# FFN gate and up projections by Strassen's seven products

## Chip, core and metric

The kernel runs on one core of one Trainium2 chip. The time is that of the device for one execution, in microseconds; lower is better. Where a profile is shown, it is one execution recorded by the hardware profiler. TensorE is called PE, VectorE DVE, ScalarE ACT, GpSimd POOL, and the engine that issues most DMAs is SyncE, SP.

## What is computed

Two groups of 256 tokens with 1024 channels (512 tokens in all) pass through a trunk of two layers. Each layer is a half-step SwiGLU FFN, a token mixer, and a second half-step FFN. All data are float32. Per layer, cut to what matters here:

```
def swiglu(x, wg, wu, wd):
    return (jax.nn.silu(x @ wg) * (x @ wu)) @ wd          # wg, wu: 1024 x 2816; wd: 2816 x 1024

x = x + 0.5 * swiglu(rmsnorm(x, ffn1_norm[l]), ffn1_wg[l], ffn1_wu[l], ffn1_wd[l])
h = rmsnorm(x, mix_norm[l])
...                                                       # gated DeltaNet and differential attention on h @ w_in[l]
x = x + merged @ w_out[l]
x = x + 0.5 * swiglu(rmsnorm(x, ffn2_norm[l]), ffn2_wg[l], ffn2_wu[l], ffn2_wd[l])
```

So there are four FFNs, two in each layer.

## The kernel before

**Precision.** PE multiplies in the format fp32r, which keeps fewer bits than float32. Every operand is therefore split into a high part (rounded to fp32r) and a low part (what is left), and a product is the sum of three matmuls: high x high, high x low, low x high. `split` (L199 to L211) does this for weights: ACT casts the high part into a tile `wh` (L208), DVE subtracts it from the float32 weights into `wl` (L210). These tiles come from the pool `pw`, which has 4 buffers of each kind.

**Loads.** `wraw` (L190) issues one load of 1 MB from SP into a tile `raw`, of which there are 2 buffers; `wcols` loads 256 columns of a weight and splits them into two blocks of 128.

**A projection.** `proj` (L218 to L224) multiplies one block of 128 weight columns with the tokens: 8 blocks of 128 channels, three matmuls each, the weights standing in the array and up to 512 token columns moving through. The normalised tokens stand transposed in `xth` and `xtl`, [128, 8, 512], channels on the partitions. The result is one PSUM bank.

**The FFN.** `ffn` (L316) walks over the 22 blocks of 128 features in two chunks of 12 and 10, two blocks (a pair) at a time: gate and up weights of the pair are loaded and split, four projections follow, and `gate` (L317 to L323) makes silu(gate) x up and splits it into `hh` and `hl`. After each chunk `rowproj` (L270) multiplies with the chunk's rows of wd and adds into the token rows `x` (L281). The first pair of an FFN does its four projections for token group 0 first and then for group 1 (256 columns at a time), since group 1's normalised tokens are complete later. `norm_T` (L244) computes them: squares on ACT (L237), the scale on POOL (L229), transposes on PE (L260), high part on ACT (L263), low part on DVE (L264).

**What sets the order.** A scheduler lays the instructions of each engine out before the run, by readiness in its own model of time and by priority: program order, or ahead of it by an offset where the text says `high_priority` (AHEAD = 1500 for loads and splits). On the chip each engine then works its queue in that order and waits on semaphores; a tile's buffer is handed on when its last reader is done. So instructions of different projections can stand interleaved on PE.

**One accumulating DMA is there already**: L553, in the mixer, adds 512 KB from DRAM onto an SBUF tile, issued by POOL.

## Time and profile before

| | |
|---|---|
| median of 3 runs | 2378.45 us (2377.96 to 2379.27) |
| the profiled execution | 2379.84 us, span of its records 2378.1 us |
| PE busy | 2342.1 us, 98% of the span |
| DVE, ACT, POOL busy | 45%, 35%, 10% |
| moved by DMA | 242.36 MB, 102 GB/s on average |

How to read it: the span is cut by instruction records, engine by engine. "Busy" is the time in which an instruction of that engine was under way; matmuls are pipelined, so one begins before the last has ended, and the step from start to start tells their rate. PEld is the load of the standing operand, which runs beside the matmuls. An idle time is put down to what ended it (the releaser). A DMA's landing is the time from its issue to its completion. Names such as wh or raw are the program's tiles without their numbers, L208 a line of the kernel.

### The profile page before, as it was taken

To read this page: it belongs to the slowest core of one execution; us is meant where nothing else is said; L and a number is where in the kernel's file an instruction comes from. 1 tells how busy PE (TensorE), PEld (TensorE's weight loads), DVE (VectorE), ACT (ScalarE), POOL (GpSimd) and SP (SyncE) were. 2 spreads that over 40 slices of the span, in tenths; PEclk is the share of its full clock that TensorE was granted. 3 is DMA by queue.
4 is the path that set the end of the run, shared out by engine and by line. 5 is a ranking of instruction groups with operands and counts; after the bars stand their busy time and mean duration, and the time that the engine had idled before them with its cause. 6 is when DMAs were issued, how large, how long until landed. Compare 5 with 4: busy or idle time off the path is not lost.

```text
span 2378.1 us, 29279 instructions
## 1 busy us (share of the span) xinstructions
PE 2342.1 (98%) x12017; PEld 1992.6 (84%) x12017; DVE 1078.5 (45%) x1716; ACT 820.7 (35%) x1593; POOL 239.5 (10%) x235
## 2 busy tenths in 40 slices
PE   7999999999999999999999999999999999999998
PEld 7888888887899888888888888888878988888887
DVE  4333334677665433333343333356776554332333
ACT  4222234744433332222332222347344333322221
POOL 1000000124351000000000000001343400000000
PEclk9999999999999999999999999999999999999999
DMA  5323234732123223233323232356321242232322
GB/s 164 106 89 104 91 124 142 176 115 78 36 72 118 96 89 103 93 97 98 106 73 106 89 107 89 124 152 172 95 83 45 63 142 89 90 105 89 106 80 80
DMA packets 210390, 242.36 MB, mean 102 GB/s; under 512 B 15565, under 2 KB 175585, under 8 KB 210256
## 3 DMA queue, kind: packets, MB, share of 16 engines
q1 hardware_dynamic: 204800, 221.96, 29.4%
q0 software_dynamic: 5280, 18.33, 3.1%
q8 instruction: 94, 1.54, 0.3%
q14 instruction: 40, 0.33, 0.0%
q10 hardware_dynamic: 176, 0.20, 0.0%
HBM read 229.17 MB, written 11.30 MB: 101 GB/s over the span
## 4 chain that ended last, share of the span: by engine, by line
PE 91%; DVE 4%; DMA 2%; ACT 2%; issue 1%; SPq 0%; POOL 0%; DVEq 0%; POOLq 0%; ACTq 0%
PE ps L222 18%; PE ps L223 18%; PE ps L224 18%; PE ps L275 8%; PE ps L277 8%; PE ps L276 8%; PE ps L730 1%; PE ps L827 1%; PE ps L935 1%; PE ps L936 1%; PE ps L937 1%; PE ps L638 1%; DMA v<-gcd 1%; PE ps L860 1%; PE ps L397 1%
## 5 line engine op out<-in xcount | busy, mean ns | idle before, releaser
L222 PE MATMUL ps<-xth,wh 128*128 128x512 f32 (+1 forms) x2208 | 827.7, 378 | 5.1 <-ACT xth L263 2.7
L223 PE MATMUL ps<-xtl,wh 128*128 128x512 f32 (+1 forms) x2208 | 829.7, 377 | 1.8 <-DVE xtl L264 1.8
L224 PE MATMUL ps<-xth,wl 128*128 128x512 f32 (+1 forms) x2208 | 827.2, 377 | 0.0
L208 ACT CAST wh<-raw 128x1024 fp32r<-128x1024 f32 x366 | 384.6, 1051 | 1065.2 <-PE ps L223 744.3
L210 DVE TENSOR_TENSOR wl<-raw,wh 128x1024 fp32r<-128x1024 f32 x354 | 440.1, 1244 | 674.3 <-ACT wh L208 659.9
L222 PEld LDWEIGHTS ps<-xth,wh 128*128 128x128 f32 x2208 | 416.9, 189 | 80.8 <-ACT xth L263 4.4
L223 PEld LDWEIGHTS ps<-xtl,wh 128*128 128x128 f32 x2208 | 418.1, 189 | 73.9 <-DVE xtl L264 2.4
L224 PEld LDWEIGHTS ps<-xth,wl 128*128 128x128 f32 x2208 | 418.0, 189 | 73.0
L276 PE MATMUL ps<-wl,u 128*128 128x512 f32 x576 | 224.4, 389 | 0.0
L275 PE MATMUL ps<-wh,u 128*128 128x512 f32 x576 | 224.3, 390 | 0.0
L277 PE MATMUL ps<-wh,u 128*128 128x512 f32 x576 | 223.2, 390 | 0.0
L320 DVE TENSOR_TENSOR t<-t,ps 128x512 f32<-128x512 f32 x88 | 60.5, 688 | 267.7 <-PE ps L224 264.3
L277 PEld LDWEIGHTS ps<-wh,u 128*128 128x128 f32 x576 | 108.2, 188 | 22.5
L275 PEld LDWEIGHTS ps<-wh,u 128*128 128x128 f32 x576 | 108.2, 188 | 22.3
L276 PEld LDWEIGHTS ps<-wl,u 128*128 128x128 f32 x576 | 108.2, 188 | 22.3
L229 POOL TENSOR_TENSOR nr<-nst,mhalf 128x1 f32<-128x1 f32 x28 | 15.5, 555 | 940.9 <-DVE nst L241 940.9
L281 DVE SCALAR_TENSOR_TENSOR u<-ps,u 128x512 f32<-128x512 f32 x80 | 53.7, 688 | 78.0 <-PE ps L277 78.0
L237 ACT ACTIVATE P<-u 128x512 f32<-128x512 f32 x56 | 35.3, 631 | 117.8 <-DVE u L281 113.3
L361 POOL DMA_DIRECT2D xs<-u x8 | 4.6, 574 | 705.9 <-DVE u L281 705.9
L935 PE MATMUL ps<-u,wh 128*128 128x256 f32 x256 | 70.4, 285 | 1.9 <-DVE u L955 1.9
L936 PE MATMUL ps<-u,wh 128*128 128x256 f32 x256 | 71.3, 287 | 0.0
L937 PE MATMUL ps<-u,wl 128*128 128x256 f32 x256 | 70.3, 285 | 0.0
(292 smaller groups left out, 2558.0 us busy)
## 6 DMA issues: line engine op xcount, KB each, us to landing
raw<-in_ffn_wg_dram SPq DMA_DIRECT2D x44, 1024.0 KB, 5.3
raw<-in_ffn_wu_dram SPq DMA_DIRECT2D x44, 1024.0 KB, 5.3
raw<-in_w_in_dram SPq DMA_DIRECT2D x44, 1024.0 KB, 5.4
raw<-in_ffn_wd_dram SPq DMA_DIRECT2D x40, 1024.0 KB, 5.0
v<-in_masks_dram SPq DMA_DIRECT2D x16, 512.0 KB, 7.1
v<-gcd POOLq DMA_DIRECT2D x16, 512.0 KB, 9.9
raw<-in_w_out_dram SPq DMA_DIRECT2D x8, 1024.0 KB, 4.9
raw<-in_ffn_wd_dram SPq DMA_DIRECT2D x8, 512.0 KB, 3.7
```

Source lines behind the costliest of these rows:

```text
L208: A.copy(hi, rv)
L210: (G_ if share and turn[0] % 2 else V).tensor_tensor(lo, rv, hi.bitcast(F32), op=ALU.subtract)
L222: T.matmul(o, wh[:, k, m], xh[:, k, c0:c1], start=k == 0, stop=False)
L223: T.matmul(o, wh[:, k, m], xl[:, k, c0:c1], start=False, stop=False)
L224: T.matmul(o, wl[:, k, m], xh[:, k, c0:c1], start=False, stop=k == n - 1)
L275: T.matmul(ps, sh[:, a], wh, start=k == 0, stop=False)
L276: T.matmul(ps, sh[:, a], wl, start=False, stop=False)
L277: T.matmul(ps, sl[:, a], wh, start=False, stop=k == nk - 1)
L320: V.tensor_tensor(s, s, pu_, op=ALU.mult)
L935: T.matmul(ps[:, c], wh[:, k, m], h_, start=k == 0, stop=False)
L936: T.matmul(ps[:, c], wh[:, k, m], l_, start=False, stop=False)
L937: T.matmul(ps[:, c], wl[:, k, m], h_, start=False, stop=k == H - 1)
```

## The change

**The products.** Except for the first pair of each FFN, a pair's gate and up projections become one 2 x 2 block product by Strassen's scheme (in the form with shared sums). The weights' quarters are wg and wu (256 columns of each) by upper and lower half of the channels; the tokens' quarters are the two halves of the channels by the two token groups. Seven products of a [512 x 256] weight combination with a [512 x 256] token combination replace eight. Each product is 2 feature blocks x 4 channel blocks x 3 split terms of matmuls with 256 moving columns. The products are summed in three PSUM tiles X, E and Z, some with further terms added on PE (`start=False`) after DVE has read what stood there.

**Weight sums.** Two of them are made by DMAs of POOL that add onto an SBUF tile: wu's upper rows onto wu's lower rows (`t3`, two tiles), and wu's upper rows onto wg's upper rows in the loaded tile `w11`, after product 1's parts have been taken from it. DVE makes `t2` from `w11` and `w22`, and later adds `w21` to it.

**Token sums.** `combos`, once per FFN after the first pair's projections: copies of the four quarters by SP, the low parts added by accumulating DMAs of POOL, four subtractions on DVE, splits on ACT and DVE. Two of the combinations overwrite token group 1's quarters in `xth` and `xtl`.

**Chunks** of the features are now 8, 8 and 6 blocks, so `rowproj` runs three times per FFN.

**The start.** The first pair's weights are loaded in quarters (`raw0`) ahead of the second token group; 22 matmuls of zeros (`spin`) run before the tokens are there and 2 more in `norm_T`; group 1's squares are put behind the casts of the first weights.

The diff, cut to its core:

```diff
...
-        with tc.high_priority(offset=AHEAD // 2):
+            raw0 = []
+            for j in range(2):
+                for n in ("ffn1_wg", "ffn1_wu"):
+                    raw0.append(uv((P, 8, P)))
+                    nc.sync.dma_start(raw0[-1], I[n][0][:, j * P:(j + 1) * P].rearrange("(k p) n -> p k n", p=P))
             load_x(2)
             load_x(3)
         g1col = p1.tile([P, 16], F32, name="g1col")
...
+        idle = p1.tile([P, P], BF16, name="idle")
+        V.memset(idle, 0.0)
+        def spin(n, lhs=None, rhs=None):
+            lhs = idle if lhs is None else lhs
+            rhs = idle.rearrange("p (a b) -> p a b", a=1).broadcast_to([P, 4, P]) if rhs is None else rhs
+            ps = bank("a", tuple(rhs.shape))
+            for _ in range(n):
+                T.matmul(ps, lhs, rhs, start=True, stop=True)
+        with tc.high_priority(offset=3 * AHEAD):
+            spin(22)
...
-        def split(rv, dst=None, share=False):
+        def split(rv, dst=None, share=False, off=AHEAD):
...
-            with tc.high_priority(offset=AHEAD):
+            with tc.high_priority(offset=off):
                 A.copy(hi, rv)
...
-        def sq_half(t, d):
+        def sq_half(t, d, behind=None):
             if d == 0:
                 sq[t] = small(f"nss{t}", (2,))
+                if behind is not None:
+                    A.copy(sq[t][:, :1], behind)
             A.activation(dtmp("P", (P, TOK)), x[t][:, d * TOK:(d + 1) * TOK], AF.Square, accum_out=sq[t][:, d:d + 1])
...
-        def norm_T(g, gain, xT):
+        def norm_T(g, gain, xT, fill=None):
...
+                if fill is not None and j == 0:
+                    with tc.high_priority(offset=-40):
+                        spin(fill, a[0][:, :P], a[1])
...
-        def ffn(wg, wu, wd, xT, after, extra=None):
+        def ffn(wg, wu, wd, xT, after, extra=None, norm=None):
...
-            for f0, f1 in ((0, 12), (12, 22)):
+            xh, xl = xT
+            low, high, g0, g1 = slice(0, 4), slice(4, 8), slice(0, 256), slice(256, 512)
+            X11, X12 = [[t[:, k, g0] for t in xT] for k in (low, high)]
+            C = {}
+            def combos():
+                q = {}
+                for g, c in enumerate((g0, g1)):
+                    for k, r in enumerate((low, high)):
+                        q[g, k] = u((P, 4, 256))
+                        with tc.high_priority(offset=100):
+                            nc.sync.dma_start(q[g, k], xh[:, r, c].bitcast(F32))
+                            G_.dma_start(q[g, k], xl[:, r, c].bitcast(F32), accum_op=ALU.add)
+                sub = lambda o, i, j: V.tensor_tensor(o, i, j, op=ALU.subtract)
+                sub(q[1, 1], q[1, 0], q[1, 1])
+                sub(q[1, 0], q[1, 0], q[0, 0])
+                sub(q[0, 0], q[0, 0], q[1, 1])
+                sub(q[0, 1], q[0, 1], q[0, 0])
+                for n, f, dst in ((5, q[1, 1], [t[:, low, g1] for t in xT]), (6, q[0, 0], None), (7, q[1, 0], None), (3, q[0, 1], None)):
+                    hi, lo = C[n] = dst or [uv((P, 4, 256), F32R) for _ in range(2)]
+                    A.copy(hi, f)
+                    V.tensor_tensor(lo, f, hi.bitcast(F32), op=ALU.subtract)
+                C[4] = [t[:, high, g1] for t in xT]
+                for t in C[4]:
+                    A.activation(t, t.bitcast(F32), AF.Copy, scale=-1.0)
+            def parts_of(pieces):
+                hi = pw.tile([P, 4, 256], F32R, tag="whi", name=nm("wh"))
+                lo = pw.tile([P, 4, 256], F32R, tag="wlo", name=nm("wl"))
+                n = 4 // len(pieces)
+                for i, r in enumerate(pieces):
+                    split(r, (hi[:, n * i:n * i + n, :], lo[:, n * i:n * i + n, :]))
+                return hi, lo
+            def product(ps, w, act, start=True):
+                (wh, wl), (ch, cl) = w, act
+                for j in range(2):
+                    m, o = slice(j * P, (j + 1) * P), ps[:, j, :]
+                    for k in range(4):
+                        T.matmul(o, wh[:, k, m], ch[:, k, :], start=start and j + k == 0, stop=False, skip_group_check=True)
+                        T.matmul(o, wh[:, k, m], cl[:, k, :], start=False, stop=False, skip_group_check=True)
+                        T.matmul(o, wl[:, k, m], ch[:, k, :], start=False, stop=k == 3, skip_group_check=True)
+            def seven(f, hh, hl):
+                c = slice(f * P, f * P + 256)
+                rows = lambda w, k0, n: w[k0 * P:(k0 + n) * P, c].rearrange("(k p) n -> p k n", p=P)
+                with tc.high_priority(offset=AHEAD):
+                    r = pr.tile([P, 2048], F32, tag="raw", name=nm("raw")).rearrange("p (q k n) -> p q k n", q=2, k=4)
+                    w11, w22 = r[:, 0], r[:, 1]
+                    nc.sync.dma_start(w11, rows(wg, 0, 4))
+                    nc.sync.dma_start(w22, rows(wu, 4, 4))
+                    t3 = [dtmp(n, (P, 2, 256)) for n in "PM"]
+                    for i, t in enumerate(t3):
+                        nc.sync.dma_start(t, rows(wu, 4 + 2 * i, 2))
+                        G_.dma_start(t, rows(wu, 2 * i, 2), accum_op=ALU.add)
+                    w21 = [dtmp(n, (P, 2, 256)) for n in "RS"]
+                    for i, t in enumerate(w21):
+                        nc.sync.dma_start(t, rows(wg, 4 + 2 * i, 2))
+                sq_ = (P, 2, 256)
+                X, E, Z = bank("f", sq_), bank("d", sq_), bank("a", sq_)
+                product(X, parts_of([w11]), X11)
+                with tc.high_priority(offset=AHEAD):
+                    G_.dma_start(w11, rows(wu, 0, 4), accum_op=ALU.add)
+                    t2 = u((P, 4, 256))
+                    V.tensor_tensor(t2, w11, w22, op=ALU.add)
+                p1s, G = dtmp("C", sq_), dtmp("E", sq_)
+                A.copy(p1s, X)
+                product(E, parts_of([t2]), C[6])
+                V.tensor_tensor(G, E, p1s, op=ALU.subtract)
+                product(Z, parts_of([w11]), C[5])
+                product(E, parts_of(t3), C[7], False)
+                H, y22 = dtmp("B", sq_), tmp(sq_)
+                V.tensor_tensor(H, E, p1s, op=ALU.subtract)
+                V.tensor_tensor(y22, Z, H, op=ALU.add)
+                product(X, parts_of(w21), X12, False)
+                s0 = tmp(sq_)
+                A.activation(s0, X, AF.Silu)
+                with tc.high_priority(offset=AHEAD):
+                    for i, t in enumerate(w21):
+                        V.tensor_tensor(t2[:, 2 * i:2 * i + 2, :], t2[:, 2 * i:2 * i + 2, :], t, op=ALU.add)
+                product(Z, parts_of([w22]), C[3], False)
+                V.tensor_tensor(G, Z, G, op=ALU.add)
+                V.tensor_tensor(s0, s0, G, op=ALU.mult)
+                product(E, parts_of([t2]), C[4], False)
+                y21 = dtmp("B", sq_)
+                V.tensor_tensor(y21, p1s, E, op=ALU.subtract)
+                A.activation(y21, y21, AF.Silu)
+                V.tensor_tensor(y22, y21, y22, op=ALU.mult)
+                for v, g in ((s0, g0), (y22, g1)):
+                    hi, lo = hh[-1][:, :, g], hl[-1][:, :, g]
+                    A.copy(hi, v)
+                    V.tensor_tensor(lo, v, hi.bitcast(F32), op=ALU.subtract)
+            for f0, f1 in ((0, 8), (8, 16), (16, 22)):
                 hh, hl = [], []
                 for f in range(0, f1 - f0, 2):
-                    mem = u if f < 10 else uv
-                    hh.append(mem(dt=F32R))
-                    hl.append(mem(dt=F32R))
-                    gs = wcols(wg, (f0 + f) * P)
-                    us = wcols(wu, (f0 + f) * P)
-                    if f0 + f == 0:
-                        bs = [bank_alt() for _ in range(4)]
+                    hh.append(u(dt=F32R))
+                    hl.append(u(dt=F32R))
+                    if f0 + f:
+                        seven(f0 + f, hh, hl)
+                        continue
+                    bs = [bank_alt() for _ in range(4)]
+                    if norm is not None:
+                        ws = []
+                        norm(0)
+                        for i, (b, rv) in enumerate(zip(bs, raw0)):
+                            hi = pw.tile([P, 8, P], F32R, tag="whi", name=nm("wh"))
+                            lo = pw.tile([P, 8, P], F32R, tag="wlo", name=nm("wl"))
+                            if i:
+                                k = (3, 7, 7)[i - 1]
+                                A.copy(hi[:, 0, :1], xT[0][:, k, :1])
+                                V.tensor_copy(lo[:, 0, :1], xT[1][:, k, :1])
+                            ws.append(split(rv, (hi, lo), off=0 if i else AHEAD))
+                            proj(b, ws[-1], xT, 0, 256)
+                        norm(1, [w[0][:, 0, :1].bitcast(F32) for w in ws])
+                        for b, w in zip(bs, ws):
+                            proj(b, w, xT, 256, 512)
+                    else:
+                        gs, us = wcols(wg, 0), wcols(wu, 0)
                         for g in range(2):
                             for b, w in zip(bs, (gs[0], us[0], gs[1], us[1])):
                                 proj(b, w, xT, g * 256, g * 256 + 256)
-                        for j in range(2):
-                            gate(bs[2 * j], bs[2 * j + 1], f + j, hh, hl)
-                    else:
-                        for j in range(2):
-                            pg, pu_ = bank_alt(), bank_alt()
-                            proj(pg, gs[j], xT)
-                            proj(pu_, us[j], xT)
-                            gate(pg, pu_, f + j, hh, hl)
+                    combos()
+                    for j in range(2):
+                        gate(bs[2 * j], bs[2 * j + 1], f + j, hh, hl)
...
-        for g in range(2):
+        def first_norm(g, behind=()):
             for t in (2 * g, 2 * g + 1):
-                sq_half(t, 0)
+                sq_half(t, 0, behind[t] if behind else None)
                 sq_half(t, 1)
-            norm_T(g, gaincol(0, 0), xT)
+            norm_T(g, gaincol(0, 0), xT, 2 if g == 0 else None)
...
-            ffn(I["ffn1_wg"][l], I["ffn1_wu"][l], I["ffn1_wd"][l], xT, to_norm(1, l), load_params if l == 0 else None)
+            ffn(I["ffn1_wg"][l], I["ffn1_wu"][l], I["ffn1_wd"][l], xT, to_norm(1, l), load_params if l == 0 else None,
+                first_norm if l == 0 else None)
...
```

## Rows read from the trace of the kernel before

**Rows 1.** Page, part 1: busy time (share) and instructions of each engine.

```profile
PE 2342.1 (98%) x12017; PEld 1992.6 (84%) x12017; DVE 1078.5 (45%) x1716; ACT 820.7 (35%) x1593; POOL 239.5 (10%) x235
```

**Rows 2.** Page, part 4: engines on the chain that ended last.

```profile
PE 91%; DVE 4%; DMA 2%; ACT 2%; issue 1%; SPq 0%; POOL 0%; DVEq 0%; POOLq 0%; ACTq 0%
```

**Rows 3.** Windows, FFN stretch: length, busy time per engine (instructions), clock, DMA share, GB/s.

```profile
60.00:280.00 220.00, 220.00 (x972) 182.29 (x971) 72.41 (x77) 56.51 (x68) 0.00 (x0) 1.00 0.31 98
```

**Rows 4.** Timeline of PE (start, duration): first and last of 28 matmuls, 512 columns.

```profile
1239.72 0.39 PE L224 MATMUL ps<-xth,wl 128*128 128x512 f32 x1
...
1245.84 0.39 PE L224 MATMUL ps<-xth,wl 128*128 128x512 f32 x1
```

**Rows 5.** Same view, 256 columns: three of L222 together; first and last of 129.

```profile
29.75 0.52 PE L222 MATMUL ps<-xth,wh 128*128 128x256 f32 x3
...
30.71 0.28 PE L222 MATMUL ps<-xth,wh 128*128 128x256 f32 x1
...
46.07 0.28 PE L223 MATMUL ps<-xtl,wh 128*128 128x256 f32 x1
```

**Rows 6.** Lines by form: shapes, count | busy us, mean ns | idle before, releaser.

```profile
L210 DVE TENSOR_TENSOR wl<-raw,wh 128x1024 fp32r<-128x1024 f32 x354 | 440.1, 1244 | 674.3 <-ACT wh L208 659.9 <-PE ps L386 9.6 <-PE ps L224 3.9
...
L320 DVE TENSOR_TENSOR t<-t,ps 128x512 f32<-128x512 f32 x88 | 60.5, 688 | 267.7 <-PE ps L224 264.3 <-PE ps L165 3.4
...
L567 DVE TENSOR_TENSOR v<-v,ua 128x1024 f32<-128x1024 f32 x8 | 9.6, 1220 | 8.2 <-ACT v L559 8.2
...
L208 ACT CAST wh<-raw 128x1024 fp32r<-128x1024 f32 x366 | 384.6, 1051 | 1065.2 <-PE ps L223 744.3 <-PE ps L277 247.9 <-PE ps L936 39.7
...
L322 ACT CAST u<-t 128x512 fp32r<-128x512 f32 x80 | 49.7, 622 | 0.9 <-DVE t L320 0.9
```

**Rows 7.** DMA issues, us to landing: L553 alone (5.2 twice), all sixteen; a plain load.

```profile
v<-gcd POOLq DMA_DIRECT2D x1, 512.0 KB, 5.2
...
v<-gcd POOLq DMA_DIRECT2D x1, 512.0 KB, 5.0
...
v<-gcd POOLq DMA_DIRECT2D x1, 512.0 KB, 6.3
...
v<-gcd POOLq DMA_DIRECT2D x16, 512.0 KB, 9.9
...
raw<-in_ffn_wd_dram SPq DMA_DIRECT2D x8, 512.0 KB, 3.7
```

**Rows 8.** Windows while one accumulate runs alone; last columns: clock, DMA share, GB/s.

```profile
476.00:477.00 1.00, 1.00 (x6) 0.84 (x5) 1.00 (x2) 0.00 (x0) 0.00 (x0) 1.00 1.05 209
```

**Rows 9.** Waits: who waited for whom, us in total, times, longest.

```profile
ACT wh L208 <- PE ps L223: 744.3, 206, 8.0
```

**Rows 10.** Timeline of DVE at the third FFN: tokens complete; first pair ends.

```profile
1204.34 3.22 DVE L264 SCALAR_TENSOR_TENSOR xtl<-ps,g1col,xth 128x256 fp32r<-128x256 f32 x8 [3.03 <-ACT xth L263]
...
1223.19 0.69 DVE L320 TENSOR_TENSOR t<-t,ps 128x512 f32<-128x512 f32 x1 [0.76 <-PE ps L224]
```

**Rows 11.** Timeline of PE at the start: dense from here; first 512-column matmul.

```profile
19.74 0.58 PE L223 MATMUL ps<-xtl,wh 128*128 128x256 f32 x1 [1.17 <-DVE xtl L264]
...
46.31 0.40 PE L222 MATMUL ps<-xth,wh 128*128 128x512 f32 x1
```

**Rows 12.** Same stretch: slow steps, their end, six transposes; granted clock (windows).

```profile
20.34 0.42 PE L222 MATMUL ps<-xth,wh 128*128 128x256 f32 x1
...
24.18 0.42 PE L222 MATMUL ps<-xth,wh 128*128 128x256 f32 x1
...
25.85 0.37 PE L223 MATMUL ps<-xtl,wh 128*128 128x256 f32 x1
...
26.41 0.82 PE L260 MATMUL ps<-cst,R 128*128 128x128 f32 x6
...
20.00:25.00 5.00, 5.00 (x24) 5.00 (x25) 2.71 (x9) 1.26 (x5) 1.69 (x3) 1.00 0.80 269
```

**Rows 13.** Timeline of ACT at the start: first square of token group 1.

```profile
17.96 0.66 ACT L237 ACTIVATE P<-u 128x512 f32<-128x512 f32 x1
```

## Prediction

> **What bounds the kernel now.** Read the busy table first: TensorE 98% against 45% on VectorE (DVE) and 35% on ScalarE (ACT) [rows 1]. The chain that ended last runs 91% over PE [rows 2]. But "busy" is no proof of a full array, so read a stage next: in the feed-forward stretch from 60 to 280 us PE never pauses, DVE is busy 72.4 of 220 us, ACT 56.5, POOL nothing, the DMA engines 0.31 [rows 3]. Here only less PE time can help. The price of a matmul is not its 390 ns duration but the step from start to start: 28 matmuls of 512 columns, 6.12 us from first to last, 0.2267 us each [rows 4]; 129 of 256 columns, 15.36 us, 0.1200 us each [rows 5]. The difference, 0.1067 us, is 256 columns at 2.4 GHz; 0.0133 us per matmul is fixed and is paid however narrow it is.
>
> **1. The products.** A pair of feature blocks (256 columns of gate and of up) takes today 2 projections x 2 blocks x 8 row blocks x 3 split terms = 96 matmuls of 512 columns: 96 x 0.2267 = 21.8 us. Strassen takes 7 products x 2 x 4 x 3 = 168 of 256 columns: 168 x 0.1200 = 20.2 us. So 1/8 fewer columns give back only 1.6 us (7%), since the fixed part is paid 168 times. The first pair of each of the 4 FFNs stays as it is, so 10 pairs x 4 = 40 change: **-64 us** at most, if PE never waits. It waits for nothing today because DVE and ACT have twice the time they need; that cover is what the change spends.
>
> The Trainium skill says, in "TensorE: Matmul & The Clock Gate", section "Back-to-back issue gap", that in streams of weight load and matmul the step is about 131 ns at 512 columns and 81 ns at 128. In proportion between these, an estimate from that page, 256 columns would step at about 98 ns, and a pair would go from 12.6 to 16.4 us: the change would cost 155 us. The rows above do not agree with either figure, and they decide; what is true in it is that narrow matmuls pay their fixed part more often.
>
> **2. The other engines in a pair** [rows 6]. DVE today: 4 low parts x 1.244 + 4 x 0.69 = 7.7 us of 21.8. DVE after: 5 low parts of 1024 elements x 1.244, 4 of 512 x 0.69, the sum t2 1.22, its second sum 2 x 0.69, seven combinations x 0.69, two low parts of the result x 0.69 (512-element rows stand for all of these): 6.2 + 2.8 + 1.2 + 1.4 + 4.8 + 1.4 = 17.8 us of 20.2, 88%. ACT: 5 x 1.05 + 9 of 512 elements x 0.62 = 10.8 us, 54%. Loads: 2 MB plain and 1 MB accumulating in place of 2 MB. The stretch moved 98 GB/s at a share of 0.31 [rows 3], so 316 GB/s at full use: 6.6 us for 2 MB. No engine is over the PE's 20.2 us, but DVE is near it.
>
> **3. The wait that the change adds.** Product 1 needs w11; then POOL's DMA adds wu's upper rows onto the same buffer; then DVE makes t2 of it, t2 is split, and product 2 needs that. An accumulating DMA is in the trace already: L553 adds 512 KB onto a tile. Alone it lands 5.0 to 6.3 us after its issue, four such cases; the median of all sixteen, most of them queued behind each other, is 9.9 [rows 7]. While one ran alone the engines were full at 209 GB/s [rows 8], two thirds of the 316 above, so 1 MB takes them 5.0 us and a pair 11.6 of 20.2 us.
>
> How early may this begin? The split tiles have 4 buffers, and ACT's casts wait today mostly for PE to give one back [rows 9]; so product 1's split comes when the product four places before it is done, and product 2 starts 4 x 24 x 0.120 = 11.5 us later. In series, with the durations of [rows 6]: cast 1.05, low part 1.24, accumulate 5.1, sum 1.22, cast 1.05, low part 1.24 less the 0.24 that the first two matmuls cover: 10.7 us. It fits by 0.8 us if no step queues. Three of them queue on a DVE that is 88% busy with operations of 0.7 to 1.2 us, and the issue on POOL queues behind the two accumulates of t3; some 0.45 us a step, 1.4 us in all, so I take **0.6 us of PE wait**. The first changed pair after a down projection is spared (its splits each feed 24 matmuls x 0.2267 = 5.4 us, so four give 21.8 us of lead): 8 of 10 pairs wait, 32 in all: **+19 us**. Bounds: 0, since the order on PE is not the program's (the matmul of L223 runs ahead of L222 in places, three of one line in a row [rows 5], and other products can fill the gap), and 173 us, where it lands as late as that median: 9.9 - 5.1 on top of 0.6, 5.4 us a pair, x 32. I stay by the lone row since POOL issues only three of these per 20 us.
>
> The Trainium skill, "DMA: Bandwidth & Descriptors", section "Anatomy of one DMA — SWDGE (gpsimd) path", fits 2.0 us plus the bytes over 436 GB/s to such a DMA. For 512 KB that is 3.2 us, an estimate from the page; the lone accumulates take 5.0 and more, so trace and page differ. By the page this wait would vanish, and the sum would be 2317.
>
> **4. The combinations of the tokens** (once per FFN): 4 plain copies and 4 accumulates of 512 KB, 4 subtractions and 4 splits on DVE (4 x 1.22 + 4 x 1.24 = 9.8 us), 6 operations on ACT. At the start of the third FFN the second token group is complete at 1207.6, and the first pair ends just before its last gating, at 1223.2 [rows 10]. From 1207.6: copies 3.7 (as a plain 512 KB load [rows 7]), two accumulates about 7.6 (5.1 and 2.5 behind it), three subtractions 3.7: 1222.6. The parts for product 5 overwrite tokens that the first pair reads, so ACT casts from 1223.2 on, product 6's operand second: ready about 1226.5 where product 1 ends at 1226.1. With the first pair's gating queued on DVE too I take 2 us per FFN, **+8 us** (bounds 0 and 24: 6 us each if all of the DVE work were exposed). The down projection in 3 chunks instead of 2 adds 8 evacuations of 0.688 us on DVE per FFN and no matmul; DVE has two thirds of that stage free: 0.
>
> **5. The start.** Dense matmuls begin at 19.7 us and the first pair ends at 46.3 [rows 11]; 19 of them from 20.34 step at 0.2133 us, the pace of 256 columns at 1.2 GHz, up to 25.8 us; the granted clock reads 1.00 there, so the step tells it, not that column [rows 12]. ACT puts group 1's squares (17.96) between the parts of group 0 [rows 13]. The zero products run while PE has nothing else, the quarters of weights come early, and the squares move behind the casts. Six us at half pace cost 3; some 2 us of order come on top: **-5 us** (bounds 0 and -8: 192 x 0.120 plus 32 transposes x 0.11 [rows 12] after a start at 12 would end at 38.6). Moved on SP: two x loads fall behind four weight loads; they are needed only for group 1.
>
> **Sum.** The profiled run took 2379.84 us (span 2378.1): -64 + 19 + 8 - 5 = -42, 2337.8; the median of the runs lies 1.4 lower: **2336 us**.
>
> **Rivals.**
> - *All hidden* (2311 us, 0.25): the order on PE fills every gap; terms 3 and 4 fall to 0 and 2. For it: the rows out of order [rows 5]. Against: under 1 us of slack.
> - *The accumulate decides, slower* (2413 us, 0.17): shared with 2 MB of plain loads per pair it lands after 7.5 us, a wait of 3.0 us x 32 = 96 in place of 19. The point: the gain is spent when the wait reaches 61 / 32 = 1.9 us, which is a landing at 6.4 us. One lone case took 6.3.
> - *DVE's queue* (2381 us, 0.10): DVE works in order; if the sum t2 stands at its head for 4.0 of the 5.1 us that the DMA is under way, waiting and 17.8 us of work make 21.8 us, and a pair lasts what it lasted.
> - *Narrow matmuls don't keep their step* (2397 us, 0.03): 21.8 / 168 = 0.1295 us is the point; at 0.132 a pair costs 0.4 us more than today, x 40 = +16 in place of -64 and +19. Against: 129 rows at 0.1200.
>
> **How the numbers follow.** Forecast 0.45. Range: 2304 (all hidden, the start at -8, term 4 at 0, 2 us for the spread of runs) to 2395, a landing near 6.9 us, which leaves out most of the slower rival. A measurement can tell some 0.2%, 5 us, from no change. Faster: 0.45 + 0.25 + part of DVE's queue = 0.76; same 0.07; slower 0.17.
>
> **What would show it.** 168 matmuls per pair at 0.120 us; product 1 to product 1 in 20.2 us if hidden, 20.8 as forecast, 21.8 without gain. PE's idle time inside a chunk put down to t2's split (DVE or its cast), and behind it to the accumulate; landing near 5 us; DVE at some 85% in the pairs; PE idle under 10 us at each FFN's second pair; the first pair ending near 41 us. I am wrong if landing exceeds 6.4 us, if DVE waits at the head of its queue for a DMA, or if steps exceed 0.1295.

## The result and the profile after

The changed kernel takes 2536.11 us (median of 4 runs, 2534.26 to 2539.42) against 2378.68 us for the kernel before: a ratio of 1.0664 [1.0651, 1.0677], 157 us slower. The forecast was 2336 us and faster. Line numbers from here on are those of the changed kernel, unless a line is said to be of an experiment.

The page of the changed kernel, busy time, granted clock in 40 slices, and the engines on the chain that ended last:

```profile
PE 2357.6 (93%) x14923; PEld 2133.0 (84%) x14923; DVE 1498.2 (59%) x2304; ACT 1000.4 (40%) x1864; POOL 415.7 (16%) x371
...
PEclk8899999999999989999989989999999999899999
...
PE 75%; DVE 11%; DMA 6%; ACT 4%; issue 3%; POOL 1%; SPq 1%; POOLq 0%; DVEq 0%; ACTq 0%
```

Against [rows 1, 2], PE fell from 98% to 93% busy and from 91% to 75% of the chain, and the clock has slices at 8. So PE waits, and at times runs at its lower level. A busy sum can't part the two, so PE's time is counted from start to start of its matmuls. Columns at 2.4 GHz plus the 0.0133 us of [rows 4, 5] count as work. What a step takes beyond that counts as slow steps, or as standstill where it is more than 0.35 us. In us, for the four FFNs together (the whole PE stream for the mixers):

| kernel | time | work | slow steps | standstill |
|---|---|---|---|---|
| before | 2378.7 | 1449 | 12 | 11 |
| changed | 2536.1 | 1391 | 66 | 163 |

Work fell by 58, slow steps grew by 54, standstill by 152; the two mixers grew by 11 (their stages, 446.5 and 445.6 to 454.0 and 449.4) and the first matmul starts 4.5 us earlier: +154 us, and the spans of the two profiles differ by 154.0 (2532.1 against 2378.1). So slow steps and standstill are more than the whole loss. Of the slow steps, 7 of the 12 us before and 51 of the 66 after are steps at just the pace of 1.2 GHz; the other 15 of the 66 are smaller delays, 9 of them in the four steps behind a stop.

**Where PE stands.** The waits of the changed kernel (engine and tile, who was waited for: us in all, times, longest):

```profile
DVE E L431 <- PE ps L391: 148.4, 40, 5.5
...
PE ps L389 <- ACT wh L226: 129.0, 55, 17.0
...
ACT wh L226 <- DVE u L414: 91.0, 29, 9.5
...
DVE u L414 <- DMA raw<-in_ffn_wu_dram: 62.8, 9, 11.6
```

Read from the second line down: PE waits for a cast, the cast (29 times) for the sum t2 on DVE (L414), but t2 waits for the accumulating transfer only 9 times in 40 pairs. By landing times it had landed ahead of t2 in 29 of the others: by 0.2 to 5.5 us, in half of them by no more than 1.1, 47 us in all. So it was the queue that held t2 there, though in half of these pairs the transfer would have let it start only some 1 us earlier. The first line tells what DVE did meanwhile: 40 times it stood at L431, which needs product 6. One pair shows it, one of the worse (3.3 of these us); DVE from the timeline (start, duration, then line, operation, and in brackets the idle time before it):

```profile
220.07 0.69 DVE L423 TENSOR_TENSOR t<-ps,B 128x512 f32<-128x512 f32 x1
226.30 0.69 DVE L431 TENSOR_TENSOR E<-ps,E 128x512 f32<-128x512 f32 x1 [5.54 <-PE ps L391]
227.10 0.69 DVE L432 TENSOR_TENSOR t<-t,E 128x512 f32<-128x512 f32 x1
227.98 0.69 DVE L435 TENSOR_TENSOR B<-C,ps 128x512 f32<-128x512 f32 x1 [0.19 <-PE ps L391]
228.58 0.68 DVE L441 TENSOR_TENSOR u<-t,u 128x512 fp32r<-128x512 f32 x1
229.18 1.22 DVE L414 TENSOR_TENSOR u<-raw 128x1024 f32<-128x1024 f32 x1
```

The same pair on ACT, POOL (the issue of the accumulate) and PE:

```profile
216.34 1.05 ACT L226 CAST wh<-raw 128x1024 fp32r<-128x1024 f32 x1 [1.79 <-PE ps L390]
...
230.44 1.04 ACT L226 CAST wh<-u 128x1024 fp32r<-128x1024 f32 x1 [1.11 <-DVE u L414]
...
218.95 1.30 POOL L412 DMA_DIRECT2D raw<-in_ffn_wu_dram  x1 [3.47 <-DVE wl L228]
...
227.66 0.28 PE L391 MATMUL ps<-xth,wl 128*128 128x256 f32 x1
231.53 0.58 PE L389 MATMUL ps<-v,wh 128*128 128x256 f32 x1 [3.59 <-ACT wh L226]
231.91 0.41 PE L390 MATMUL ps<-v,wh 128*128 128x256 f32 x1
```

And that transfer among the DMA issues of this stretch, with its time to landing:

```profile
raw<-in_ffn_wu_dram POOLq DMA_DIRECT2D x1, 512.0 KB, 7.0
```

It landed at 218.95 + 7.0 = 225.95. DVE had idled since 220.8 in front of L431, which waits for the old pair's product 6; then it worked off three more sums and gates of that pair, and t2 came at 229.18. From the split's cast to product 2 it took 15.2 us, not the 10.7 of the prediction, and PE stood for 3.6.

**And the clock.** The same stretch in windows (length, busy time of PE, PEld, DVE, ACT, POOL, granted clock, DMA share, GB/s):

```profile
231.50:236.00 4.50, 4.32 (x18) 4.02 (x19) 4.49 (x6) 3.53 (x6) 0.00 (x0) 0.50 0.01 2
236.00:240.00 4.00, 4.00 (x30) 4.00 (x29) 3.84 (x6) 1.05 (x1) 1.05 (x2) 0.80 0.71 200
240.00:245.00 5.00, 5.00 (x44) 5.00 (x44) 1.35 (x3) 1.22 (x2) 1.38 (x2) 1.00 0.93 234
```

After the stop the granted clock is 0.50, that is 1.2 GHz. The first three matmuls step at 0.38 to 0.57 us, the next 22 at 0.213 instead of 0.120: 2.6 us of slow steps on top of the 3.6. The pair lasted 26.3 us from product 2 to product 2 (205.26 to 231.53), where 20.8 were forecast.

**The second pair of an FFN** waits for the token combinations, in the first FFN 17 us at one go (PE, timeline):

```profile
59.67 0.58 PE L389 MATMUL ps<-xth,wh 128*128 128x256 f32 x1 [17.00 <-ACT wh L226]
```

The copies and their accumulates land late (page, DMA issues: count, KB, median us to landing):

```profile
u<-xth SPq DMA_DIRECT2D x16, 512.0 KB, 11.3
u<-xtl POOLq DMA_DIRECT2D x16, 512.0 KB, 9.6
```

### The profile page after: what moved, and what is told of

Same layout as the page of the kernel before. It is cut to its first block, busy times and chain, and to the rows that moved or that the text cites. A ratio compares the mean times of both kernels' runs of the same rounds, so it can differ in the third digit from the quotient of the medians.

```text
span 2532.1 us, 36917 instructions
## 1 busy us (share of the span) xinstructions
PE 2357.6 (93%) x14923; PEld 2133.0 (84%) x14923; DVE 1498.2 (59%) x2304; ACT 1000.4 (40%) x1864; POOL 415.7 (16%) x371
## 4 chain that ended last, share of the span: by engine, by line
PE 75%; DVE 11%; DMA 6%; ACT 4%; issue 3%; POOL 1%; SPq 1%; POOLq 0%; DVEq 0%; ACTq 0%
PE ps L389 10%; PE ps L391 10%; PE ps L390 10%; PE ps L298 7%; PE ps L299 7%; PE ps L300 7%; PE ps L241 4%; PE ps L240 4%; PE ps L242 4%; DVE wl L228 2%; DMA u<-xth 2%; ACT wh L226 2%; PE ps L859 1%; DMA v<-gcd 1%; PE ps L956 1%
## 5 line engine op out<-in xcount | busy, mean ns | idle before, releaser
L389 PE MATMUL ps<-xth,wh 128*128 128x256 f32 x1280 | 373.2, 292 | 60.7 <-ACT wh L226 58.9
L391 PE MATMUL ps<-xth,wl 128*128 128x256 f32 x1280 | 366.2, 286 | 9.6 <-DVE wl L228 9.6
L390 PE MATMUL ps<-xtl,wh 128*128 128x256 f32 x1280 | 367.8, 287 | 0.0
L389 PE MATMUL ps<-v,wh 128*128 128x256 f32 x960 | 292.7, 305 | 72.5 <-ACT wh L226 70.1
L240 PE MATMUL ps<-xth,wh 128*128 128x512 f32 (+1 forms) x928 | 326.8, 361 | 6.0 <-ACT t L499 2.0
L241 PE MATMUL ps<-xtl,wh 128*128 128x512 f32 (+1 forms) x928 | 329.9, 361 | 1.0 <-DVE xtl L287 1.0
L242 PE MATMUL ps<-xth,wl 128*128 128x512 f32 (+1 forms) x928 | 327.4, 358 | 0.0
L391 PE MATMUL ps<-v,wl 128*128 128x256 f32 x960 | 289.0, 301 | 0.0
L390 PE MATMUL ps<-v,wh 128*128 128x256 f32 x960 | 288.3, 300 | 0.0
L389 PEld LDWEIGHTS ps<-v,wh 128*128 128x128 f32 x960 | 202.1, 210 | 79.1 <-ACT wh L226 75.8
L390 PEld LDWEIGHTS ps<-v,wh 128*128 128x128 f32 x960 | 202.2, 211 | 0.4
L391 PEld LDWEIGHTS ps<-v,wl 128*128 128x128 f32 x960 | 202.3, 211 | 0.2
```

Of the source, the lines that this page charges most:

```text
L240: T.matmul(o, wh[:, k, m], xh[:, k, c0:c1], start=k == 0, stop=False)
L241: T.matmul(o, wh[:, k, m], xl[:, k, c0:c1], start=False, stop=False)
L242: T.matmul(o, wl[:, k, m], xh[:, k, c0:c1], start=False, stop=k == n - 1)
L389: T.matmul(o, wh[:, k, m], ch[:, k, :], start=start and j + k == 0, stop=False, skip_group_check=True)
L390: T.matmul(o, wh[:, k, m], cl[:, k, :], start=False, stop=False, skip_group_check=True)
L391: T.matmul(o, wl[:, k, m], ch[:, k, :], start=False, stop=k == 3, skip_group_check=True)
```

## The experiments

**Take the two waits away (e1, e2, e3).** The theory was then that the transfer behind t2 holds each pair. e1 loads wu's upper rows plainly and early and lets POOL add:

```diff
+  w12 = u((P, 4, 256))
+  nc.sync.dma_start(w12, rows(wu, 0, 4))
+  G_.tensor_tensor(w12, w12, w11, op=ALU.add)
...
-  G_.dma_start(w11, rows(wu, 0, 4), accum_op=ALU.add)
-  V.tensor_tensor(t2, w11, w22, op=ALU.add)
+  V.tensor_tensor(t2, w12, w22, op=ALU.add)
...
-  product(Z, parts_of([w11]), C[5])
+  product(Z, parts_of([w12]), C[5])
```

> The upper rows of wu are loaded plainly, ahead, into a tile of their own and summed there by GpSimd; nothing of the pair waits any more for the cast of product 1. The waits at the second product of a pair are the main part of the lost time (theory: of the 152 us of idle TensorE in the four FFNs some 90 stand there, and most of the 54 us of steps at the lower clock follow them): 2536 minus 90 to 130, 2405 to 2445 us. If the token combinations hold most of it (rival 1), under 30 us go: 2505 or more. If GpSimd's slower sum comes late itself, or the loads' traffic is the limit, 2480 to 2530. Idle of TensorE ahead of the second product: under 0.6 us per pair where it was 2.3 to 3.8.

Measured: 2577.8 us, 42 more than the changed kernel, where the theory gave 2405 to 2445; standstill 163 to 194 in the FFNs. The theory in that form fell. e2 takes the combinations' copies off the DMA queues:

```diff
-  nc.sync.dma_start(q[g, k], xh[:, r, c].bitcast(F32))
-  G_.dma_start(q[g, k], xl[:, r, c].bitcast(F32), accum_op=ALU.add)
+  (V if g else G_).tensor_tensor(q[g, k], xh[:, r, c].bitcast(F32), xl[:, r, c].bitcast(F32), op=ALU.add)
```

> The token combinations take the sum of the high and low part directly on GpSimd and VectorE, without the copy and the accumulating transfer; the sums by accumulating transfer of the pairs stay. Theory: the stops at each FFN's second pair (17 + 1.4 + 4.8 us in the first FFN, 11 + 1.5 + 2 in the others) fall by about half: 2536 minus 25 to 45, 2490 to 2510 us. If GpSimd's four engine sums take as long as the transfers did: within 10 us of 2536. If the combinations held most of the loss (rival 1), 2450 or less.

Measured: 2476.9 us, 59 less, more than expected. The first FFN's stop fell from 17.0 to 6.0 us (PE timeline of e2):

```profile
50.20 0.58 PE L388 MATMUL ps<-v,wh 128*128 128x256 f32 x1 [6.03 <-ACT wh L226]
```

Both together:

> Both edits of the two runs before. Theory: nothing in the steady pairs waits, and the clock holds: 2536 minus 120 to 190, 2345 to 2415 us, thus near the kernel before or below it; the products alone give 64 us on 2378.7, less 8 to 15 per FFN at the second pair. Rival (a third cause, VectorE's queue or the narrow steps, holds the pair at 22 us or more whatever the sums do): 2440 or more.

Measured: 2531.6 us (2526.9 to 2533.4), in the range of the rival, a third cause that holds the pair whatever the sums do.

**Is it the accumulate, or t2's place? (e7, e5, e6).** e7 takes only the accumulate off the in-place transfer. It leaves the sum of w11 and wu's upper rows out, so it computes something else and serves for its time alone:

```diff
-  G_.dma_start(w11, rows(wu, 0, 4), accum_op=ALU.add)
+  G_.dma_start(w11, rows(wu, 0, 4))
```

> The in-place transfer of the upper rows of wu loses only its accumulate: the same 512 KB from the same queue after the same wait, landing plainly in place of being added (the sum w11+w12 is left out). It prices the accumulate against a plain landing. If accumulating itself is slow, the landing falls from 6.0 to about 4 us and the 31 interior waits fall by about 2 us each with it, 2536 minus 50 to 90, 2445 to 2485 us. If t2 waits in VectorE's queue and not for the landing, the time stays within 15 us of 2536.

Measured: 2531.1 us, 5 less, as expected if t2 waits in the queue. The plain landing (DMA issues of e7) is 4.1 us where the accumulate takes 6.0, and this buys nearly nothing:

```profile
raw<-in_ffn_wu_dram POOLq DMA_DIRECT2D x40, 512.0 KB, 4.1
```

By the fit in the Trainium skill, "DMA: Bandwidth & Descriptors", section "Anatomy of one DMA — SWDGE (gpsimd) path", the estimate for such a transfer is 3.2 us. Plain it is 0.9 us above that here, accumulating 2.8.

e5 makes t2 from w11 and t3, whose two accumulates are issued a pair ahead, and lets the in-place accumulate follow; e6 adds e2's edit.

```diff
+  for i, t in enumerate(t3):
+      V.tensor_tensor(t2[:, 2 * i:2 * i + 2, :], w11[:, 2 * i:2 * i + 2, :], t, op=ALU.add)
...
   G_.dma_start(w11, rows(wu, 0, 4), accum_op=ALU.add)
...
-  V.tensor_tensor(t2, w11, w22, op=ALU.add)
```

> The first sum t2 of a pair (w11+w12+w22) is made from w11 and the already landed sum t3 (w12+w22), ahead of the in-place accumulate, so that only product 3 waits for that transfer, one product later. The run with plainly loaded rows said little of the wait, since its two tiles per pair shared the two free buffers of the u ring and the sum came behind the old pair's last gate instead. Theory (the wait at the second product is the accumulate's chain plus VectorE's queue): the idle of 1.8 to 3.8 us per interior pair goes, about 85 of the 187 us of idle, and some 20 to 40 us of the lower clock behind it: 2536 minus 85 to 125, 2410 to 2450 us. Rival (VectorE's in-order queue holds t2 whatever it reads): 2500 or more.

> The run before together with the token combinations on the engines (which alone took 59 us off). Theory: both stops go, 2536 minus 60 minus 85 to 125, 2350 to 2391 us: about the kernel before, with the shorter products visible. Rival (a queue is late whatever is summed where): 2440 or more.

Measured: 2604.3 us (68 more) and 2541.5 us (2541.3 to 2541.8). Both miss, and the timeline of e6 says why (DVE, then POOL's issue of the in-place accumulate):

```profile
214.56 0.69 DVE L431 TENSOR_TENSOR E<-ps,E 128x512 f32<-128x512 f32 x1 [4.41 <-PE ps L390]
...
217.34 0.68 DVE L413 TENSOR_TENSOR u<-raw,P 128x512 f32<-128x512 f32 x1
217.94 0.69 DVE L413 TENSOR_TENSOR u<-raw,M 128x512 f32<-128x512 f32 x1
...
219.17 1.30 POOL L414 DMA_DIRECT2D raw<-in_ffn_wu_dram  x1 [10.81 <-DVE u L413]
```

t2 (here L413) follows L431 with no wait of its own: DVE stood 4.41 us in front of L431. And now POOL's transfer stands behind t2 (10.81 us), so product 3 is late as well. What t2 reads is not the point; where it stands in DVE's queue is. In e5's expectation the failure of e1 is laid to the buffers of the u ring; no run tried that. The queue is enough to explain e1: in the 28 pairs with an older pair ahead of them t2 starts 2.9 us (median) after L431 in the changed kernel, but 4.8 us after that line's counterpart in e1 and 4.9 in e3, behind the last gate too (in e3 at 221.97). These 2 us a pair come to some 50, where e1 lost 42; what put t2 behind the last gate is not shown.

**Change the order in the queue (e9).** The scheduler lays out by readiness in its own model, by priority and by program order; the changed kernel asks for t2 with a high priority, and it still ends up behind the gates. e9 writes the next pair's loads, first split, accumulate and t2 into the program ahead of the old pair's last sums:

```diff
-  def seven(f, hh, hl):
+  def prep(f):
...
-      product(X, parts_of([w11]), X11)
...
+      w1 = parts_of([w11])
       G_.dma_start(w11, rows(wu, 0, 4), accum_op=ALU.add)
       t2 = u((P, 4, 256))
       V.tensor_tensor(t2, w11, w22, op=ALU.add)
...
+  def seven(f, hh, hl, pre, nxt_f):
+      w1, w11, w22, t3, w21, t2 = pre or prep(f)
...
+      product(X, w1, X11)
...
       product(Z, parts_of([w22]), C[3], False)
-      V.tensor_tensor(G, Z, G, op=ALU.add)
-      V.tensor_tensor(s0, s0, G, op=ALU.mult)
       product(E, parts_of([t2]), C[4], False)
...
+      nxt_pre = prep(nxt_f)
+      V.tensor_tensor(H, Z, G, op=ALU.add)
+      V.tensor_tensor(s0, s0, H, op=ALU.mult)
```

> All of the change as it is, its two accumulating transfers and its copies included, but the next pair's loads, first split, in-place accumulate and sum t2 are written into the program ahead of the old pair's last sums and gates, so that in VectorE's queue t2 stands ahead of the instructions that wait for products 6 and 7. Nothing is summed elsewhere. Theory now (VectorE's in-order queue holds t2, not the transfer: the plain landing took 5 us off, and t2 made from tiles that had long landed was no earlier): the waits at the second products go, some 80 us of idle with 10 to 40 us of lower clock behind it, 2536 minus 80 to 120, 2416 to 2456 us. Rival (the accumulate's chain of 10.7 us against 11.5 us of lead, as predicted): the sum is then at the head of VectorE's queue and blocks it until the transfer lands; 2500 or more.

Measured: 2462.7 us, 73 less with the same transfers, 7 short of its range; ratio to before 1.0352 [1.0337, 1.0368]. The standstill in the FFNs falls from 163 to 114, the slow steps from 66 to 46. A pair on DVE (L411 is t2, L439 the old L431):

```profile
209.95 0.69 DVE L427 TENSOR_TENSOR t<-ps,B 128x512 f32<-128x512 f32 x1
216.37 1.22 DVE L411 TENSOR_TENSOR u<-raw 128x1024 f32<-128x1024 f32 x1 [5.73 <-DMA raw<-in_ffn_wu_dram]
218.71 1.23 DVE L228 TENSOR_TENSOR wl<-u,wh 128x1024 fp32r<-128x1024 f32 x1 [1.11 <-ACT wh L226]
219.85 0.68 DVE L439 TENSOR_TENSOR B<-ps,E 128x512 f32<-128x512 f32 x1
```

And a line of its waits:

```profile
DVE u L411 <- DMA raw<-in_ffn_wu_dram: 207.2, 36, 10.2
```

Now t2 does stand at the head and waits for the transfer in 36 pairs, 207 us in all, and the kernel is faster for it: PE needs t2 next, and L439 only later. What e9 tests is the order of the whole preparation, not t2 alone. In the pairs shown the in-place accumulate is issued 3.3 us before ACT copies product 1 out, in both kernels, and only t2 has moved against it. In other pairs the issue came some 4 us earlier or later against that copy: it waits for the split's low part, which stands in DVE's queue too.

**What is left then (e10, e11).** e10 adds e2's edit. e11 also makes t2 from t3, as e5 did; the first split and the accumulate, which must then follow t2, go back to `seven`.

> The order of the run before, and the token combinations on the engines, which alone took 59 us off. Theory: 2536 minus 59 minus 80 to 120, 2357 to 2397 us, thus about the kernel before. If less than 10 us of idle per FFN is left, the clock's extra 59 us is the whole of what remains against the forecast of 2336.

> As the run before, but t2 made from w11 and the landed t3, ahead of the in-place accumulate, which then only product 3 waits for. If VectorE's queue was all of it, this is within 10 us of the run before, 2350 to 2395 us; if the accumulate still holds the second product there, this one is 20 us or more faster than it.

Measured: 2410.7 us, 1.0129 [1.0107, 1.0152], missing its expectation by 14; and **2362.4 us, 0.9931 [0.9916, 0.9946]: 0.7% faster than the kernel before**. e11 is 48 us under e10, so the accumulate did hold product 2 once the queue no longer hid it. The busy line of its page:

```profile
PE 2302.2 (98%) x14923; PEld 2086.0 (88%) x14923; DVE 1513.6 (64%) x2352; ACT 997.4 (42%) x1864; POOL 412.3 (17%) x363
```

And the largest of PE's waits in it, 18 us where the changed kernel had 129:

```profile
PE ps L388 <- ACT wh L226: 18.2, 13, 6.0
```

The same t3 edit cost 68 us with t2 behind the gates (e5) and gave 48 with t2 ahead of them (e11). The count of PE's time over the four FFNs, in the order in which the causes were taken away:

| kernel | time | work | slow steps | standstill |
|---|---|---|---|---|
| changed | 2536.1 | 1391 | 66 | 163 |
| e2: combinations | 2476.9 | 1391 | 67 | 106 |
| e9: queue order | 2462.7 | 1391 | 46 | 114 |
| e10: order, combinations | 2410.7 | 1391 | 44 | 64 |
| e11: and t2 from t3 | 2362.4 | 1391 | 25 | 37 |

**The clock (e4, e12, e13, e14).** e2 took 57 us of standstill and no slow steps; the other edits took both. Is a standstill the cause of the lower clock at all? e4 puts ten matmuls of zeros ahead of each second product of the changed kernel.

> Ten matmuls of zeros (0.227 us each at the full clock, 2.3 us in all) stand ahead of the second product of each of the 40 pairs, in the time in which TensorE was idle for 2.6 to 3.6 us; the sums wait as before. Theory that the idle itself brings the clock down: the steps at 0.213 us behind the second product's start go, some 30 to 50 us in all, 2490 to 2510 us. Rival (the clock falls for another reason, as a budget over a longer time, and the idle has nothing to do with it): the time stays or grows, 2530 to 2600.

Measured: 2561.8 us, 26 more, in the range of the rival. Over the whole stream the zeros add 91 us of work and take 50 of 187 us of standstill and 7 of 177 us of slow steps: 34 more, and the spans differ by 33.4 (2565.5 against 2532.1). These sums don't decide it, since the zeros delay more than they fill; single pairs say more. In four pairs 24 zeros run in one block of 5.0 us, in four others 14 in 2.8 us, with no stop beside them. Behind each of these eight blocks one matmul steps at 0.31 us, and the following ones keep 0.120. One such block (timeline and windows of e4):

```profile
207.47 5.35 PE L419 MATMUL ps<-idle 128*128 128x512 bf16 x24
...
207.50:212.50 5.00, 5.00 (x27) 2.29 (x25) 4.43 (x7) 4.88 (x8) 0.00 (x0) 1.00 0.00 0
212.50:217.00 4.50, 4.50 (x39) 4.47 (x38) 3.22 (x7) 1.05 (x1) 0.85 (x1) 1.00 0.65 188
```

e12 and e13 start from e11, which has few such stops, and are meant to put a stop, or zeros of the same length, there:

```diff
   w2 = parts_of([t2])
+  for _ in range(2):
+      A.copy(E, X)
   product(E, w2, C[6])
```

```diff
   w2 = parts_of([t2])
+  for _ in range(13):
+      T.matmul(E.rearrange("p a b -> p (a b)"), idle, idle.rearrange("p (a b) -> p a b", a=1).broadcast_to([P, 4, P]),
+               start=True, stop=True)
   product(E, w2, C[6])
```

> The run with the order, the combinations and t2 from t3 (2362 us), with two copies of product 1's result into product 2's bank on ScalarE ahead of the second product of each of the 40 pairs: TensorE stands still there for some 2.5 to 3 us, as it did in the changed kernel, and nothing else is added to it. Theory (each such stop is followed by steps at the lower clock, by the other traces 1.4 to 3 us of them whatever its length): idle of 100 to 120 us more, and 50 to 80 us more of steps at the lower clock: 2362 plus 150 to 200, 2512 to 2562 us. Rival (the lower clock has another cause, and the stops of the changed kernel only stood near it): the idle alone, 2462 to 2482 us.

> The same kernel with thirteen matmuls of zeros (13 by 0.2267, 2.95 us) in the place of each of these stops: TensorE is as long away from its work, but not still. Theory: 2362 plus 40 by 2.95, 118, 2480 us within 8, and the steps at the lower clock stay at the 134 us of the run without them. Rival (it is the time away from the products, not the standstill, or a budget): 2500 or more.

e12: 2364.8 us; standstill 62 us over the stream where e11 has 59, because PE went on with other products: product 1 ended at 220.9 us and product 2 began at 226.9, with 0.49 us of standstill ahead of it. e12 made no stop and tells nothing of one. e13: 2443.6 us; 118 us more work, slow steps 120 us (e11: 134), standstill 36 (59). It misses its 2480 on the good side, since the zeros also give the sums time. On PE the 13 zeros of a pair mostly run in two blocks, of 0.7 to 1.8 us, so e13 is a weaker test than it was meant to be; but behind its three blocks of 20, which last 4.1 us, no matmul steps at the pace of 1.2 GHz either. The last zero of a block counts as too short a step, which takes some 18 us off the slow steps; those at just the pace of 1.2 GHz cost 9 us in the FFNs, in e11 15. Its clock in a window of 150 us:

```profile
170.00:320.00 150.00, 150.00 (x1034) 135.98 (x1034) 90.64 (x114) 53.76 (x69) 16.21 (x13) 1.00 0.51 126
```

e14 makes true stops, by copies on DVE through the banks of products 2 and 3:

```diff
   w2 = parts_of([t2])
+  with tc.high_priority(offset=AHEAD):
+      V.tensor_copy(Z, X)
+      V.tensor_copy(E, Z)
+      V.tensor_copy(Z, E)
+      V.tensor_copy(E, Z)
   product(E, w2, C[6])
```

> The run before the last made no stops: the second copy wrote only product 2's bank, product 3 went ahead of it, and TensorE did not stand still (62 us of idle, 59 without the copies). Here four copies on VectorE go from product 1's result through the banks of products 2 and 3, so that no product of the pair can run before they end, 2.5 to 4 us per pair. Theory (a standstill is followed by steps at the lower clock): idle of 100 to 160 us more, and 50 to 90 us more of steps at the lower clock, 2510 to 2610 us; in the trace the stops are followed by steps at 0.21 us. Rival: the steps at the lower clock stay at 120 to 135 us in all, as they did with the zeros, and the time grows by the idle alone.

Measured: 2594.4 us. Against e11 the FFNs have 165 us more standstill (202), just over the 160 expected, and 60 us more slow steps (85), 54 of them at just the pace of 1.2 GHz; the time is within its range. One stop, and what follows it (windows of e14):

```profile
230.30:237.50 7.20, 0.14 (x2) 0.00 (x0) 6.67 (x11) 4.07 (x8) 0.82 (x2) 0.76 0.26 77
237.50:241.50 4.00, 4.00 (x21) 4.00 (x22) 2.08 (x3) 0.00 (x0) 1.61 (x2) 0.58 0.98 208
241.50:246.00 4.50, 4.50 (x40) 4.50 (x39) 1.93 (x3) 2.09 (x2) 0.00 (x0) 1.00 0.35 60
```

PE is busy for 0.14 of 7.2 us; then 21 matmuls take 4.0 us, and from 241.5 on 40 take 4.5. Away from its work but busy (the blocks of e4 and e13) PE keeps 2.4 GHz; standing still (e14) it falls to 1.2 GHz: the standstill is the cause.

**The start alone (e8).** The kernel before with the quarter loads, the zero products and the new order of the first norm:

```diff
+  raw0.append(uv((P, 8, P)))
+  nc.sync.dma_start(raw0[-1], I[n][0][:, j * P:(j + 1) * P].rearrange("(k p) n -> p k n", p=P))
...
+  spin(22)
...
+  norm(0)
...
+      proj(b, ws[-1], xT, 0, 256)
+  norm(1, [w[0][:, 0, :1].bitcast(F32) for w in ws])
```

> The kernel before with the start of the change alone: the first pair's weight columns loaded as four tiles at highest priority, the products of zeros ahead of the tokens, the second half of the norm behind the first projections; the 512-column projections and everything after them as before. Theory: the 7 us by which the first pair ended earlier in the changed kernel (39.3 against 46.0) are kept to the end: 2378.7 minus 4 to 8, 2371 to 2375 us. Rival (the rest of the FFN was waiting for its loads and gives the gain back): 2377 to 2380 us.

Measured: 2376.5 us against 2379.5, 0.9986 [0.9977, 0.9994]: -3 us, between the theory and the rival. Matmul by matmul the profiled run is 5.5 us ahead from 43 us on, and 2.0 at the end; the rest went in the mixers. Why is open.

## Why the prediction failed, point by point

- **Step 1, the products: right.** Work in the FFNs fell by 58 us, and the start's filler matmuls add 5.9 (e8: 2223.6 against 2217.7 us over the stream), so the pairs gave 64, as forecast. Work is a count at a fixed price, so the steps have to bear it out: of the 6720 matmuls of the products 6112 step at 0.120 us in the changed kernel (466 at 0.213), and 6601 in e11. The rival of narrow matmuls that don't keep their step is out.
- **Step 2, the other engines: the sums were right, and misled.** The pair of the changed kernel from 205.2 to 231.5 us has 16.6 us of DVE and 10.1 of ACT where 17.8 and 10.8 were forecast; nothing is overfull. A load of 88% was read as delay of some 0.45 us a step. The delay that came was not from load: DVE idled 148 us in front of L431.
- **Step 3, the wait for the in-place sum: the step that failed.** The chain of durations nearly held: cast 1.05, low part 1.23, sum 1.22, cast 1.04, and a median of 6.0 us of landing against 5.1. The rival "the accumulate decides" had its point at 6.4; 11 of the 40 landings passed it, the median did not, and landing 2 us earlier gave only 5 us (e7). What failed is "three of them queue on a DVE that is 88% busy": t2 queued behind instructions that themselves wait for products 6 and 7 of the pair before. Such a chain starts when PE is nearly through with the old pair, and so all of its tail is PE's wait. Putting the next pair's preparation ahead of these instructions gave 73 us (e9); the term itself, what the transfer costs at the right place, is 48 us (e10 to e11) against the 19 of the forecast: 27 of standstill, 20 of slow steps.
- **The rival "DVE's queue"** had the engine right and the order the wrong way round: it had t2 at the head, blocking the rest. The changed kernel shows that picture, the sign of being wrong that the prediction named, in 9 of 40 pairs (62.8 us); in e9 it is the rule, and e9 is the faster kernel.
- **Step 4, the combinations: mis-sized.** 8 us, bounds 0 and 24; taking the copies off the DMA queues gave back 59 (e2) or 52 (e9 to e10). The step priced a copy at the 3.7 us of a plain load [rows 7]. Six of the sixteen landed like that, in 3.3 to 4.5 us; the other ten, all four of the first FFN among them, took 11.0 to 15.1. The accumulates onto them took 5.8 to 14.0, and POOL's queue takes them one behind the other, each waiting for its copy.
- **Step 5, the start: right at the start.** -5 forecast, -5.5 at 43 us, but only -3 at the end (e8).
- **A missing term: the clock.** 54 us of slow steps, 45 of them at just the pace of 1.2 GHz. The prediction used the slow steps of the start [rows 12] for the start alone, and never asked what a new stop in the middle would do to the matmuls behind it.
- **The remainder.** e11 has work -58.2, standstill +25.5, slow steps +12.6, mixers +7.6 and an earlier first matmul -4.5: -17.0 us; the spans differ by 17.1 (2361.0 against 2378.1). The gain of the products is real, and the FFN's second pair still stops for 6 us in the first FFN.

## What to carry to other kernels

When an edit puts an operation on an engine that works in order, ask what stands ahead of it in that queue and what each of these waits for; how busy the engine is says nothing about it. A sum that the next block needs belongs, in the program, ahead of the last steps of the old block, since a priority alone did not bring it there. And price each new stop of PE as the stop plus the slow steps behind it, here 1.8 us in the mean.

## What the runs showed of the hardware

- The loss at the clock goes far more by the number of stops than by their length. Count standstills over 1 us that are no more than 2 us apart as one stop, and the slow steps of the 8 us behind it as its cost. Over the FFNs of ten traces (the changed kernel, e1 to e3, e5 to e7, e9 to e11) that gives 257 stops of 1.6 to 23 us, which cost 1.8 us in the mean: 1.5 behind the 69 shortest (under 2 us) and 2.3 behind the 17 over 13 us. So e2, which has 30 such stops of 2.7 us in the mean where the changed kernel has 33 of 4.3, took hardly any slow steps away.
- An accumulating transfer of 512 KB from DRAM lands 6.0 us after its issue (median of 40) where the same transfer lands plainly in 4.1 (e7). Copies of 512 KB from tile to tile landed in 3.3 to 4.5 us or in 11.0 to 15.1, where plain loads of 512 KB of wu from DRAM took 5.5 in the middle; what parts the two groups was not followed up.
